# Seven half-size products for eight in the down projections of a two-layer encoder

## Chip, cores and metric

One Trainium2 chip, one core. The time is the device time of one execution in microseconds (us); of several runs the median is given. TensorE (PE in the profile) multiplies, VectorE is DVE, ScalarE is ACT, GpSimd is POOL, and SyncE (SP) here only issues transfers.

## What is computed

An encoder trunk of two layers is applied to two sequences of 512 and 256 tokens with the same weights; the kernel handles them side by side as 768 tokens of width 1024, in fp32. Each layer has an attention part and then a feed-forward part with a hidden width of 4096:

```python
for layer in range(DEPTH):                 # DEPTH = 2
    ...                                    # attention, residual add
    h = rmsnorm(x, ln_mlp[layer])
    x = x + jnp.square(jax.nn.relu(h @ w_up[layer])) @ w_down[layer]
return rmsnorm(x, ln_f)
```

The change concerns the second product of the last line, the down projection: 768 tokens x 4096 hidden features x 1024 outputs, once per layer.

## The kernel before

Activations lie with features on the 128 partitions and tokens along the columns: `x` is 8 tiles of 128 x 768. Every fp32 operand of a product is split into a high part of type fp32r (`hi`, a rounded copy by ScalarE) and the rest (`lo = src - hi`, a subtraction on VectorE): `wsplit` for weights (lines 78 to 81), `halve` for activations (lines 114 to 120). Each product is then three matmuls into the same PSUM accumulator: hi*hi, hi*lo, lo*hi. PSUM has 8 banks, 3 under the tag "mm" and 5 under "at" (`BANKS`).

`mlp(layer, ...)` holds the feed-forward part. Its up projection makes 16 pairs of hidden blocks (a block is 128 hidden features). The first two pairs are plain products. The other fourteen are made by the Strassen-Winograd scheme: tokens in two halves of 384 (`A`, `B`), input features in two halves, the two blocks of a pair as the third halving; seven products of half size in place of eight. The sums of weights that this needs are made by `weights` on GpSimd (line 866), the sums of activations once by `second` on VectorE (line 815), and the seven results are added to the outputs by VectorE (lines 889 and 952). `finish` applies ReLU, norm and square (lines 894 to 896), and the 16 results go to DRAM as `H`, of 128 x 2 x 768 each.

The down projection follows, the part that changes. The 32 hidden blocks are taken in four groups (`NG`) of eight (`GF`). For each group `read` loads the blocks two at a time on GpSimd's transfer queue (line 922) and splits them (`hp`). Then for each pair of output tiles (`mq`) two weight tiles of 128 x 1024 are loaded on SP's queue and split (`wtile`, lines 74, 80, 81), and for each output tile `proj_feat` (line 204) runs 8 blocks x 3 terms of a 512-column and a 256-column matmul (`dna`, `dnb`) on the same weights; VectorE adds both results to `x` (line 982). In layer 0's last group each finished tile of `x` is also split for the next layer and its square is summed. In layer 1 the last group is `final` (line 786): all outputs for the 512 tokens of the long sequence first, then, with the weights loaded and split a second time, for the other 256; each segment is normed, multiplied (line 795) and stored as soon as its eight tiles are there.

The kernel is written with a tile framework: buffers come from pools with a fixed number of slots per tag (`wraw` 3, `whi` and `wlo` 4 each), semaphores are added automatically, and the instructions of each engine are put into an order by a planner that follows the order in the program where several are ready. Once fixed, an engine's order is not changed on the chip: an instruction that waits holds up all behind it.

Of the kernel before, what the change touches and what calls it, by code (L numbers as in the profile page):

```python
# [17 lines left out]
P = 128  # L18
# [7 lines left out]
FF = 4 * D  # L26
NG = 4
GF = FF // P // NG
HT = NT // 2
MO = (0, 4, 1, 5, 2, 6, 3, 7)  # L30
MASKED = -3.0e38
# [6 lines left out]
def kernel(ctx: ExitStack, tc: tile.TileContext, a: dict, y: bass.AP):  # L38
# [75 lines left out]
    def halve(hi, lo, src, gain=None):  # L114
        if gain is None:
            nc.scalar.activation(hi, src, AF.Copy)  # L116
            nc.vector.tensor_tensor(out=lo, in0=src, in1=hi.bitcast(F32), op=ALU.subtract)  # L117
# [650 lines left out]

    def final(hs, x, sq):

        start = woff["w_down"]
        acc = cpool.tile([P, NT], F32, tag="acc", name="acc", bufs=1)
        R = cpool.tile([P, NT], F32, tag="R", name="R", bufs=1)
        for i, (s, e) in enumerate(SEGS):
            woff["w_down"] = start
            sl = slice(s, e)
            nm = Norm(sq, (s, e), acc)
            for mq in range(KD // 2):
                ws = [wtile("w_down", 1024) for _ in range(2)]
                for mi in range(2):  # L780
                    m = 2 * mq + mi
                    ps = ps_tile("mm", "fin")[:, : e - s]
                    lhs = down_lhs(ws, mi)
                    for k in range(GF):
                        for j, (part, mv) in enumerate(((0, hs[k][0]), (0, hs[k][1]), (1, hs[k][0]))):
                            nc.tensor.matmul(ps, lhs(k, part), mv[:, sl], start=(k == 0 and j == 0),  # L786
                                             stop=(k == GF - 1 and j == 2))
                    nc.vector.tensor_tensor(out=x[m][:, sl], in0=ps, in1=x[m][:, sl], op=ALU.add)
                    nm.add(x[m], KD - 1 if s else KD)
                    nc.scalar.activation(x[m][:, sl], x[m][:, sl], AF.Copy, scale=gcol(G_F, m))  # L790
            nm.spread(nm.rstd(), R)
            for k in range(KD):
                yt = x[k][:, sl]
                eng = nc.gpsimd if k % 3 == 1 else nc.vector
                eng.tensor_tensor(out=yt, in0=yt, in1=R[:, sl], op=ALU.mult)
                (nc.sync, nc.scalar)[k % 2].dma_start(y[:, k, sl], yt)

    def mlp(layer, src, o, x, es):

        g1s, g2s, st = ExitStack(), ExitStack(), ExitStack()
# [5 lines left out]
        A, B = slice(0, HT), slice(HT, NT)  # L808

        def put(pool, c, j, src, gain=None):  # L810
            t = comb[c, j] = pool.tile([P, 2, HT], F32R, tag=f"c{c}", name=f"c{c}", bufs=4)
            halve(t[:, 0], t[:, 1], src, gain)

        def stt(out, x_, s, y_, op):
# [2 lines left out]
        def first(j):  # L817

            for c, k, tk in ((1, j, B), (0, j, A), (2, j + 4, B), (3, j + 4, A)):
                put(g1, c, j, x[k][:, tk], gcol(g, k))  # L820

        def second():

# [13 lines left out]

        run(out_proj(src, o, None, x, 1, first))
        es.close()
        g2 = g2s.enter_context(tc.tile_pool(name="g2", bufs=4, side="right", reuse_waits="tile"))  # L840
        up = g2s.enter_context(tc.tile_pool(name="up", bufs=3, side="right", reuse_waits="tile"))

        def weights(plain=False):

# [7 lines left out]
            if plain:  # L852
# [7 lines left out]
            sa, sb = (up.tile([P, 1024], F32, tag="s", name="s", bufs=3) for _ in range(2))  # L860
# [53 lines left out]
        second()  # L914
        plain(both[1])

        hs = []

        def read(pool, f):

            hr = pa_.tile([P, 2, NT], F32, tag="hr", name="hr", bufs=2)
            nc.gpsimd.dma_start(hr, H[f // 2])  # L922
            for i in range(2):
                hp = pool.tile([P, 2, NT], F32R, tag="hp", name="hp")
                halve(hp[:, 0], hp[:, 1], hr[:, i])
                hs.append((hp[:, 0], hp[:, 1]))

        for mp in range(2, FF // 256):
            w = weights()
# [9 lines left out]
                rt = nm.rstd()  # L939
            if mp == FF // 256 - 1:  # L940

                g1s.close()
                pa_ = g1s.enter_context(tc.tile_pool(name=f"dna{layer}", bufs=4, reuse_waits="tile"))
                read(pa_, 0)
                read(pa_, 2)
            add(z12, one(6), z11)
            add(z11, p2, z11)
            p4 = one(4)
# [9 lines left out]
                    finish(wait.pop(0))  # L958
            finish(z)
        g2s.close()  # L960

        es = open_hl() if layer == 0 else None
        pb_ = st.enter_context(tc.tile_pool(name=f"dnb{layer}", bufs=6, reuse_waits="tile"))
        nxt, nn = [], Norm(sq)
        for grp in range(NG):
            if grp:
                hs = []
            for f in range(len(hs), GF, 2):
                read(pa_ if grp and f in (2, 4) else pb_, grp * GF + f)
            if layer == 1 and grp == NG - 1:  # L970
                final(hs, x, sq)
                st.close()
                g1s.close()
                return
            for mq in range(KD // 2):
                ws = [wtile("w_down", 1024) for _ in range(2)]
                for mi in range(2):
                    m = 2 * mq + mi
                    pa, pb = ps_tile("mm", "dna"), ps_tile("at", "dnb")
                    run(proj_feat(down_lhs(ws, mi), hs, GF, pa, pb))  # L980
                    xm = x[m]
                    evac_halves(pa, pb, lambda ps, s: nc.vector.tensor_tensor(out=xm[:, s], in0=ps, in1=xm[:, s], op=ALU.add))  # L982
                    if grp == NG - 1:
                        nxt.append(split(xm, "x", gcol(G_O, m)))
                        nn.add(xm)
        spill = dram.tile([P, KD, NT], F32, name="spill")
        for m in range(KD):
            nc.sync.dma_start(spill[:, m, :], x[m])
        st.close()
        g1s.close()  # L990
        return es, nxt, nn, spill


    hs_ = open_hl()
# [55 lines left out]
def _layout(i):  # L1050
# [40 lines left out]
    wd = i["w_down"].reshape(2, NG, 2, 4, P, D // 256, 256)  # L1091
    d["w_down"] = wd.transpose(0, 1, 5, 2, 4, 3, 6).reshape(-1)

    d["bias"] = _bias(i["rpb"][0])
    rep = lambda v: np.broadcast_to(v, (P, *v.shape))
# [39 lines left out]
```

## Time and profile before

| | |
|---|---|
| median of three runs | 1824.62 us (1824.50 to 1825.94) |
| the profiled execution | 1822.1 us, its span 1820.1 us |
| mean granted TensorE clock | 0.992 |
| TensorE / VectorE / ScalarE / GpSimd busy | 1777.1 / 1127.7 / 764.2 / 363.5 us |
| down projection of layer 0 | from 621.2 to 892.7 us of the span |
| down projection of layer 1, with the final norm | from 1532.9 us to the end |

A profile row names the line of the kernel, the engine, the operation, the tile written and the tiles read, the shape, and the count. In grouped rows the busy time and the mean duration in ns follow, then the idle time of the engine before such instructions with what ended it; rows by tile give least, median and greatest duration. Rows in order of time begin with the start in the span and the length in us; of several equal instructions in a row the length runs from the first start to the last end. Matmuls are pipelined: the distance of their starts counts, not their duration.

### The profile page before, as it was taken

The page shows a single profiled execution, that of the slowest core. Times are in us where ns is not written, and L with a number is a line of the kernel's source. Part 1 is how long each engine was busy: PE and PEld are TensorE (multiplying, and loading weights), DVE is VectorE, ACT ScalarE, POOL GpSimd, SP SyncE. Part 2 cuts the span into 40 slices and gives each one's busy share as a digit, 9 for nine tenths or more (in the row PEclk, how much of TensorE's full clock was granted, in tenths as well). Part 3 has the DMA queues.
Part 4 walks back from the last instruction along what each step waited for, and adds up shares of the span by engine and source line. Part 5 has one row for each costly group of instructions (what it writes and reads, how often), then busy time and mean ns, then how long its engine had stood idle before and what let it go on. Part 6 is the DMA issues. An engine that isn't in the chain of part 4 may idle for free.

```text
span 1820.1 us, 28502 instructions
## 1 busy us (share of the span) xinstructions
PE 1777.1 (98%) x11358; PEld 1627.3 (89%) x11358; DVE 1127.7 (62%) x2083; ACT 764.2 (42%) x1485; POOL 363.5 (20%) x366
## 2 busy tenths in 40 slices
PE   7999999999999999999999999999989999999997
PEld 7877888899999988888999999988989999888877
DVE  7777647497766634325366776775976667343255
ACT  6665534364434412213235555554544334122143
POOL 1421000014544200000022222210235442000002
PEclk8999999999999999999999999999999999999999
DMA  5111222313333634323211110122133336343233
GB/s 166 44 33 37 68 83 88 131 35 110 139 125 130 213 111 139 119 67 122 93 51 44 47 48 22 53 68 93 36 109 140 122 125 207 126 131 124 70 99 115
DMA packets 50019, 176.70 MB, mean 97 GB/s; under 512 B 5856, under 2 KB 8672, under 8 KB 49888
## 3 DMA queue, kind: packets, MB, share of 16 engines
q1 hardware_dynamic: 38656, 121.91, 21.2%
q0 software_dynamic: 4608, 25.17, 4.1%
q10 hardware_dynamic: 6624, 27.81, 3.9%
q8 instruction: 89, 1.46, 0.3%
q14 instruction: 42, 0.34, 0.1%
HBM read 142.63 MB, written 31.46 MB: 96 GB/s over the span
## 4 chain that ended last, share of the span: by engine, by line
PE 78%; DVE 8%; issue 8%; DMA 3%; ACT 3%; POOL 1%; DVEq 0%; SPq 0%; ACTq 0%; POOLq 0%
PE up L881 23%; PE dna L204 11%; PE dqk L192 8%; PE dnb L204 6%; PE opa L204 5%; PE dvp L192 4%; PE fin L786 3%; DMA hr<-H 2%; PE opb L204 2%; PE npa L204 2%; PE ds L270 2%; PE dpv L713 2%; DVE t L815 1%; PE vp L192 1%; PE qp L192 1%
## 5 line engine op out<-in xcount | busy, mean ns | idle before, releaser
L881 PE MATMUL up<-c,whi 128*128 128x384 f32 x1824 | 468.6, 338 | 5.8 <-ACT whi L80 5.8
L881 PEld LDWEIGHTS up<-c,whi 128*128 128x128 f32 x1824 | 331.9, 189 | 6.6 <-ACT whi L80 6.5
L204 PE MATMUL dna<-hp,whi 128*128 128x512 f32 x896 | 331.8, 394 | 1.1 <-DVE hp L117 0.9
L80 ACT ACTIVATE whi<-wraw 128x1024 fp32r<-128x1024 f32 (+2 forms) x200 | 193.3, 967 | 324.5 <-PE dnb L204 222.6
L881 PE MATMUL up<-c,wlo 128*128 128x384 f32 x912 | 308.1, 339 | 2.1 <-DVE wlo L81 2.1
L81 DVE TENSOR_TENSOR wlo<-wraw,whi 128x1024 fp32r<-128x1024 f32 (+2 forms) x204 | 228.4, 1121 | 98.9 <-ACT whi L80 98.7
L204 PE MATMUL dnb<-hp,whi 128*128 128x256 f32 x896 | 250.0, 283 | 0.0
L204 PEld LDWEIGHTS dna<-hp,whi 128*128 128x128 f32 x896 | 168.1, 188 | 42.1 <-DVE hp L117 1.9
L866 POOL TENSOR_TENSOR s<-wraw 128x512 f32<-128x512 f32 x56 | 94.1, 1699 | 414.9 <-DMA wraw<-in_w_up_dram 199.8
L204 PE MATMUL dna<-hp,wlo 128*128 128x512 f32 x448 | 176.6, 394 | 0.0
L881 PEld LDWEIGHTS up<-c,wlo 128*128 128x128 f32 x912 | 172.2, 189 | 2.9 <-DVE wlo L81 2.9
L204 PEld LDWEIGHTS dnb<-hp,whi 128*128 128x128 f32 x896 | 167.2, 188 | 0.3
L889 DVE TENSOR_TENSOR z<-up,z 128x384 f32<-128x384 f32 x168 | 92.9, 553 | 90.4 <-PE up L881 79.0
L982 DVE TENSOR_TENSOR x<-dna,x 128x512 f32<-128x512 f32 x56 | 38.7, 691 | 165.6 <-PE dna L204 165.4
L204 PE MATMUL dnb<-hp,wlo 128*128 128x256 f32 x448 | 126.9, 283 | 0.0
L192 PE MATMUL dqk<-whi,xh 128*128 128x256 f32 x384 | 114.7, 299 | 0.0
L192 PE MATMUL dqk<-whi,xl 128*128 128x256 f32 x384 | 107.5, 280 | 0.0
L192 PE MATMUL dqk<-wlo,xh 128*128 128x256 f32 x384 | 107.2, 279 | 0.0
L922 POOL DMA_DIRECT2D hr<-H x32 | 17.6, 550 | 431.6 <-DVE hp L117 390.8
L204 PEld LDWEIGHTS dna<-hp,wlo 128*128 128x128 f32 x448 | 84.1, 188 | 18.3
L80 ACT ACTIVATE whi<-s 128x1024 fp32r<-128x1024 f32 x56 | 59.5, 1063 | 84.8 <-PE up L881 83.5
L116 ACT ACTIVATE hp<-hr 128x768 fp32r<-128x768 f32 x64 | 50.9, 837 | 100.2 <-PE dnb L204 61.8
(214 smaller groups left out, 3892.7 us busy)
## 6 DMA issues: line engine op xcount, KB each, us to landing
wraw<-in_w_down_dram SPq DMA_DIRECT2D x72, 512.0 KB, 3.6
wraw<-in_w_up_dram SPq DMA_DIRECT2D x64, 512.0 KB, 3.5
H<-z ACTq DMA_DIRECT2D x32, 768.0 KB, 3.3
hr<-H POOLq DMA_DIRECT2D x32, 768.0 KB, 5.9
wraw<-in_w_in_o_dram SPq DMA_DIRECT2D x24, 512.0 KB, 3.6
wraw<-in_w_in_e_dram SPq DMA_DIRECT2D x16, 512.0 KB, 3.7
x<-in_xT_dram SPq DMA_DIRECT2D x16, 384.0 KB, 5.4
nbias<-in_bias_dram SPq DMA_DIRECT2D x20, 256.0 KB, 3.8
```

Of the source, the lines that this page charges most:

```text
L80: nc.scalar.activation(hi, raw, AF.Copy)
L81: nc.vector.tensor_tensor(out=lo, in0=raw, in1=hi.bitcast(F32), op=ALU.subtract)
L116: nc.scalar.activation(hi, src, AF.Copy)
L192: nc.tensor.matmul(ps[:, :256], st[:, tk], col(k, part, 0, 256), start=(k == 0 and i == 0), stop=(k == KD - 1 and i == 2))
L204: nc.tensor.matmul(ps[:, : e - s], w, mv[:, s:e], start=(k == 0 and i == 0), stop=(k == nk - 1 and i == 2))
L270: nc.tensor.matmul(out[h], q(a_, hp, qs), k(b_, hp, ks), start=i == 0, stop=i == 2)
L713: nc.tensor.matmul(pv, pt[:, i * P : (i + 1) * P], v[:, k0 // P + i, vc], start=(i == 0), stop=(i == nk - 1))
L786: nc.tensor.matmul(ps, lhs(k, part), mv[:, sl], start=(k == 0 and j == 0), stop=(k == GF - 1 and j == 2))
L866: nc.gpsimd.tensor_tensor(out=d_, in0=x_, in1=y_, op=ALU.add)
L881: nc.tensor.matmul(ps, part[a_][:, base + k * P : base + (k + 1) * P], t[:, b_], start=q + k + i == 0, stop=q == n - 1 and k == 3 and i == 2)
L889: nc.vector.tensor_tensor(out=out, in0=x_, in1=y_, op=op)
L982: evac_halves(pa, pb, lambda ps, s: nc.vector.tensor_tensor(out=xm[:, s], in0=ps, in1=xm[:, s], op=ALU.add))
```

## The change

Per layer, hidden pairs 0, 1 and 14, 15 (the first and last four blocks) stay plain, with half as many blocks per output tile as before. The other twelve pairs, n = 0 to 11 for H[2] to H[13], go in four groups (`SG`) of three (`SJ`) by the seven-product scheme, now with the two blocks of a pair as the summed halving, the token halves, and two output tiles.

- `pair` loads the two blocks (two transfers on SP's queue), makes four sums of 128 x 384, and splits seven operands (three of 384, two of 768 that hold two operands each). The sums are on GpSimd for the first group and on VectorE afterwards. Buffers hold five pairs, so that two of the next group's three can be made while a group is in use.
- `down_weights` loads two tiles of 128 x 768, makes four sums of 128 x 384 on GpSimd, and splits four tiles (768, 384, 768, 768).
- `down_pair` runs the seven products, each summed in PSUM over the group's three pairs and the three terms (9 matmuls of 384 columns), in the order 1, 2, 6, 5, 7, 3, 4. Accumulator `u` takes 1, and after copies or reads also 6, 7 and 4; `v` takes 5 and then 3; `r` takes 2. ScalarE copies two intermediate results (`keep`), VectorE adds five to `x` from PSUM, GpSimd adds the two copies.
- Loads of `H` move from GpSimd's queue to SP's, in two halves.
- `final` has four blocks instead of eight and keeps the split weights for its second segment.
- Pools are opened and closed in another order to make room; the weight layout in DRAM follows the new order of use.

```diff
+SJ = 3
+SG = (FF // 256 - 4) // SJ
...
     def final(hs, x, sq):
...
-                ws = [wtile("w_down", 1024) for _ in range(2)]
+                if i == 0:
+                    kept.append([wtile("w_down", 1024)])
+                ws = kept[mq]
...
-                    for k in range(GF):
+                    for k in range(len(hs)):
...
+        hrp = st.enter_context(tc.tile_pool(name=f"hr{layer}", bufs=4, reuse_waits="tile"))
...
-            hr = pa_.tile([P, 2, NT], F32, tag="hr", name="hr", bufs=2)
-            nc.gpsimd.dma_start(hr, H[f // 2])
+        def load(mp):
+            hr = [hrp.tile([P, NT], F32, tag="h", name="hr", bufs=4) for _ in range(2)]
             for i in range(2):
+                nc.sync.dma_start(hr[i], H[mp][:, i])
+            return hr
...
+        def pair(n, eng):
+
+            low = n % 5 > 2
+            hr = load(n + 2)
+            b11, b12, b21, b22 = hr[0][:, A], hr[0][:, B], hr[1][:, A], hr[1][:, B]
+            t = pa_.tile([P, 3, HT], F32, tag="t", name="dt", bufs=1)
+            n6, n7, t4 = (t[:, i] for i in range(3))
+
+            def small(src, scale=None):
+                c = (pa_ if low else ph_).tile([P, 2, HT], F32R, tag="c3", name="c3", bufs=6 if low else 9)
+                halve(c[:, 0], c[:, 1], src, scale)
+                return c[:, 0], c[:, 1]
+
+            def large(pool, bufs, src):
+                c = pool.tile([P, 2, NT], F32R, tag="c6", name="c6", bufs=bufs)
+                halve(c[:, 0], c[:, 1], src)
+                return [(c[:, 0, h], c[:, 1, h]) for h in (A, B)]
+
+            d = ops[n] = {1: small(b12, -1.0)}
+            eng.tensor_tensor(out=n7, in0=b11, in1=b21, op=ALU.subtract)
+            eng.tensor_tensor(out=b11, in0=b12, in1=b11, op=ALU.subtract)
+            eng.tensor_tensor(out=n6, in0=b21, in1=b11, op=ALU.add)
+            eng.tensor_tensor(out=t4, in0=b22, in1=n6, op=ALU.subtract)
+            d[3], d[2] = large(*((pa_, 4) if low else (pm_, 3)), hr[1])
+            d[6], d[7] = large(*((pa_, 4) if low else (ph_, 3)), t[:, :2].rearrange("p a t -> p (a t)"))
+            d[5] = small(b11)
+            d[4] = small(t4)
+
+        def down_weights():
+
+            w = SJ * P
...
+            sa = xo_tile("s")
+            sb = pa_.tile([P, NT], F32, tag="s", name="s", bufs=1)
...
+            for ps_, t in (((1, 4), raws[0]), ((2,), raws[1]), ((6, 5), sa), ((7, 3), sb)):
+                if t is sa:
+                    for d_, x_, y_ in ((s1, a21, a22), (s2, s1, a11), (s3, a11, a21), (s4, a12, s2)):
+                        nc.gpsimd.tensor_tensor(out=d_, in0=x_, in1=y_, op=ALU.add)
+                hi, lo = whilo(w * len(ps_))
+                wsplit(hi, lo, t[:, : w * len(ps_)])
...
+        def down_pair(g, q, w):
+
+            xs1, xs2 = x[2 * q], x[2 * q + 1]
+            x11, x12, x21, x22 = xs1[:, B], xs1[:, A], xs2[:, B], xs2[:, A]
+            u, v, r = ps_tile("at", "du")[:, :HT], ps_tile("at", "dv")[:, :HT], ps_tile("mm", "dr")[:, :HT]
+
+            def prod(ps, n, start):
+                part, base = w[n]
+                for j in range(SJ):
+                    c = ops[g * SJ + j][n]
+                    for i, (a_, b_) in enumerate(((0, 0), (0, 1), (1, 0))):
+                        nc.tensor.matmul(ps, part[a_][:, base + j * P : base + (j + 1) * P], c[b_],
+                                         start=start and j + i == 0, stop=j == SJ - 1 and i == 2, skip_group_check=not start)
+
+            def keep(ps, scale):
+                t = ph_.tile([P, HT], F32, tag="pk", name="pk", bufs=2)
+                nc.scalar.activation(t, ps, AF.Copy, scale=scale)
+                return t
+
+            def put(xd, ps, op=ALU.add, eng=nc.vector):
+                eng.tensor_tensor(out=xd, in0=xd, in1=ps, op=op)
+
+            prod(u, 1, True)
+            p1 = keep(u, -1.0)
+            prod(r, 2, True)
+            prod(u, 6, False)
+            put(x12, u, ALU.subtract)
+            put(x11, r)
+            put(x11, p1, eng=nc.gpsimd)
+            prod(v, 5, True)
+            p5 = keep(v, -1.0)
+            prod(u, 7, False)
+            put(x22, u)
+            put(x22, p5, eng=nc.gpsimd)
+            prod(v, 3, False)
+            put(x12, v)
+            prod(u, 4, False)
+            put(x21, u)
...
+        plain_down(hs, lambda xm, m: None)
+        w = down_weights()
+        for n in range(SJ):
+            pair(n, nc.gpsimd)
+        for g in range(SG):
+            for q in range(KD // 2):
+                down_pair(g, q, down_weights() if g + q else w)
+            if g < SG - 1:
+                for n in range((g + 1) * SJ, (g + 2) * SJ):
+                    pair(n, nc.vector)
+        hs = []
+        for mp, pools in ((14, ((pm_, 3), (pa_, 4))), (15, ((pa_, 4), (pa_, 0)))):
+            read(mp, pools, hs)
```

`plain_down` is the former loop over output tiles with four blocks, and `read` now fills the plain blocks' operands from `load`.

More of the change, by code (lines that the diff above doesn't have):

```diff
@@ L859, in weights @@
                 return out
[L860 removed]
+            sa, sb = (us.tile([P, 1024], F32, tag="s", name="s", bufs=3) for _ in range(2))
             s2, s1, s3, s4 = (r[:, i * 512 : (i + 1) * 512] for r in (sa, sb) for i in range(2))
@@ new lines, in read @@
+        def read(mp, pools, hs):
+            hr = load(mp)
+            for i, (pool, bufs) in enumerate(pools):
+                if bufs:
+                    hp = pool.tile([P, 2, NT], F32R, tag="c6", name="c6", bufs=bufs)
+                    hi, lo = hp[:, 0], hp[:, 1]
+                else:
+                    hi, lo = (pool.tile([P, 2, HT], F32R, tag="c3", name="c3", bufs=6).rearrange("p a t -> p (a t)") for _ in range(2))
+                halve(hi, lo, hr[i])
+                hs.append((hi, lo))
@@ L940, in mlp @@
             if mp == FF // 256 - 1:
+                uss.close()
                 g1s.close()
                 pa_ = g1s.enter_context(tc.tile_pool(name=f"dna{layer}", bufs=4, reuse_waits="tile"))
-                read(pa_, 0)
-                read(pa_, 2)
+                hs = []
+                for mp_ in range(2):
+                    read(mp_, ((pa_, 4), (pa_, 4)), hs)
             add(z12, one(6), z11)
@@ L960, in mlp, with plain_down @@
         g2s.close()
[L962 to L974, printed above, removed]
+        pm_ = ms.enter_context(tc.tile_pool(name=f"dnm{layer}", bufs=3, reuse_waits="tile"))
+        ph_ = bs.enter_context(tc.tile_pool(name=f"dnh{layer}", bufs=3, reuse_waits="tile"))
+        def plain_down(hs, then):
             for mq in range(KD // 2):
-                ws = [wtile("w_down", 1024) for _ in range(2)]
+                ws = [wtile("w_down", 1024)]
                 for mi in range(2):
```

74 lines of the change are left out of this document (51 added, 23 removed).

## The prediction

> **What bounds the kernel now.** I read the page's shares first, then the chain that ended last, then busy times by stretch, then groups by shape, then the order in time where VectorE and GpSimd are busy at once.
>
> ```profile
> span 1820.1 us, 28502 instructions
> PE 1777.1 (98%) x11358; PEld 1627.3 (89%) x11358; DVE 1127.7 (62%) x2083; ACT 764.2 (42%) x1485; POOL 363.5 (20%) x366
> PE 78%; DVE 8%; issue 8%; DMA 3%; ACT 3%; POOL 1%; DVEq 0%; SPq 0%; ACTq 0%; POOLq 0%
> ```
>
> TensorE is busy 98% of the span and carries 78% of the last chain, so fewer columns through TensorE are worth their time as long as nothing else becomes late. The next view gives busy times in pieces of the first up, first down, second up and second down projection (length, then busy time and count for each engine).
>
> ```profile
> core 0: us, PE busy (x) PEld busy (x) DVE busy (x) ACT busy (x) POOL busy (x), PEclk, DMA share, GB/s
> 450.00:600.00 150.00, 150.00 (x861) 150.00 (x860) 104.61 (x122) 60.39 (x62) 79.80 (x43) 1.00 0.38 129
> 640.00:760.00 120.00, 120.00 (x678) 104.79 (x677) 46.83 (x62) 26.70 (x29) 4.32 (x8) 1.00 0.33 107
> 1360.00:1520.00 160.00, 160.00 (x917) 160.00 (x917) 112.68 (x134) 63.16 (x65) 81.38 (x44) 1.00 0.37 127
> 1540.00:1700.00 160.00, 159.83 (x910) 139.81 (x909) 62.49 (x80) 38.64 (x42) 5.94 (x11) 1.00 0.39 126
> ```
>
> The down stage has TensorE full at clock 1.00, VectorE 39% busy (46.83 of 120) and GpSimd idle: TensorE alone bounds it. The up stage already runs seven products for eight, with VectorE at 70% and GpSimd at 53%, and TensorE still never stops. That is the nearest sight of what the down stage will become.
>
> **The change, part by part.**
>
> *TensorE.* A 384-column product takes 150/861 = 0.1742 or 160/917 = 0.1745 us: 0.1743. A down product is a 512 and a 256 column one together: 2 x 120/678 = 0.354 or 2 x 160/910 = 0.3516, mean 0.3528. Per layer 24 of 32 blocks change. Before: 24 blocks x 8 output tiles x 3 terms = 576 pairs x 0.3528 = 203.2 us. After: 4 groups x 4 column pairs x 7 products x 3 block pairs x 3 terms = 1008 x 0.1743 = 175.7 us. Gain 27.5 per layer, 55.0 in all. The eight plain blocks keep their columns. [...]
>
> *VectorE and ScalarE.* Durations by shape (mean ns after the busy time, or least/median/most), and runs of equal instructions, which give the pitch:
>
> ```profile
> L81 DVE TENSOR_TENSOR wlo<-wraw,whi 128x1024 fp32r<-128x1024 f32 x152 | 185.7, 1223 | 97.9 <-ACT whi L80 97.8
> L117 DVE TENSOR_TENSOR hp<-hr,hp 128x768 fp32r<-128x768 f32 x64 | 58.8, 954 | 46.1 <-ACT hp L116 45.7
> L117 DVE TENSOR_TENSOR c<-t,c x32: 544/551/1655, 384.4 to 1317.9; 128x384 fp32r<-128x384 f32 x32
> L889 DVE TENSOR_TENSOR z<-up,z x168: 542/552/559, 423.1 to 1538.6; 128x384 f32<-128x384 f32 x168
> L116 ACT ACTIVATE hp<-hr 128x768 fp32r<-128x768 f32 x64 | 50.9, 837 | 100.2 <-PE dnb L204 61.8 <-DMA hr<-H 30.2 <-DMA H<-z 7.3
> 384.39 1.96 DVE L117 TENSOR_TENSOR c<-t,c 128x384 fp32r<-128x384 f32 x4
> 621.50 1.82 DVE L117 TENSOR_TENSOR hp<-hr,hp 128x768 fp32r<-128x768 f32 x2
> L936 ACT ACTIVATE z<-up x28: 470/493/495, 416.8 to 1520.5; 128x384 f32<-128x384 f32 x28
> ```
>
> Four 384-wide ones in 1.96 us, the last taking 0.55: pitch (1.96 - 0.55)/3 = 0.47. Two of 768 in 1.82: pitch 0.87 (1.82 less one of 0.95). Call a step one `down_pair` with its weights: 63 products, 10.98 us of TensorE, 16 per layer. VectorE per step: weight splits of 768, 384, 768, 768 = 3.08; five additions out of PSUM (552 ns as the 384 split's 551) 5 x 0.47 = 2.35. Per pair of hidden blocks: three 384 splits, two 768 splits, four additions = 3 x 0.47 + 2 x 0.87 + 4 x 0.47 = 5.03. Nine of twelve pairs are made during the first twelve steps, 0.75 per step, 3.77. Together 9.20 of 10.98 us, 84%: it fits, with little room. ScalarE per step: splits 3 x 0.84 + 0.49, two `keep` 0.98, pairs 0.75 x (3 x 0.49 + 2 x 0.84) = 2.4, in all 6.4: not the bound.
>
> *GpSimd.* Four weight sums and two additions into `x` per step, all 384 wide.
>
> ```profile
> 568.66 1.30 POOL L866 TENSOR_TENSOR s<-wraw,s 128x512 f32<-128x512 f32 x1
> L674 POOL TENSOR_TENSOR rope_o<-t,t x48: 457/462/1285, 915.4 to 1195.2; 128x128 f32<-128x128 f32 x48
> ```
>
> Undisturbed it takes 1.30 us for 512 columns and 0.46 for 128, so about 1.02 for 384: 6.1 of 10.98 us. Alone it fits too.
>
> *The two together.* This is what decides. GpSimd and VectorE take turns:
>
> ```profile
> 386.26 4.79 DVE L815 SCALAR_TENSOR_TENSOR t<-x,gains,t 128x384 f32<-128x384 f32 x3
> 385.26 3.81 POOL L866 TENSOR_TENSOR s<-wraw 128x512 f32<-128x512 f32 x2 [191.01 <-ACT c L116]
> 389.03 1.61 POOL L866 TENSOR_TENSOR s<-s,wraw 128x512 f32<-128x512 f32 x1
> L815 DVE SCALAR_TENSOR_TENSOR t<-x,gains,t x32: 600/611/1658, 381.7 to 1313.8; 128x384 f32<-128x384 f32 x32
> L152 DVE TENSOR_TENSOR acc<-acc,sq 128x512 f32<-128x512 f32 x7 | 4.8, 688 | 2.1 <-ACT sq L147 2.1
> 1789.65 6.38 DVE L795 TENSOR_TENSOR x<-x,R 128x512 f32<-128x512 f32 x5
> 1789.76 5.12 POOL L795 TENSOR_TENSOR x<-x,R 128x512 f32<-128x512 f32 x3 [2.08 <-DVE R L182]
> ```
>
> Three VectorE instructions with both inputs in SBUF took 4.79 us, 1.60 each where 0.61 is usual, and in the same time GpSimd made about one per 1.60. Additions that read PSUM (L889) never stretched: 542 to 559 ns over 168. So a GpSimd 512 occupies what both need for 1.60 - 0.47 = 1.13 us; in the last stage's multiplications, 512 wide (free 0.69, pitch 0.61), for (6.38 - 5 x 0.61 - 0.08)/3 = 1.08. With 1.10, a 384 takes 0.83 by columns. Per step: VectorE with two SBUF inputs 3.08 + 3.77 = 6.85, GpSimd 6 x 0.83 = 5.0, sum 11.85, above TensorE's 10.98. If GpSimd's turns all fall under the PSUM additions or idle time of VectorE the step is 11.85; if none do, 6.85 + 2.35 + 5.0 = 14.2. From below, the up stage shows the turns nearly free:
>
> ```profile
> 563.78 0.86 DVE L81 TENSOR_TENSOR wlo<-wraw,whi 128x512 fp32r<-128x512 f32 x1
> 565.14 2.28 DVE L894 SCALAR_TENSOR_TENSOR z<-z,R 128x1536 f32<-128x1536 f32 x1
> 607.80 0.69 DVE L81 TENSOR_TENSOR wlo<-wraw,whi 128x512 fp32r<-128x512 f32 x1
> 608.99 1.76 DVE L894 SCALAR_TENSOR_TENSOR z<-z,R 128x1536 f32<-128x1536 f32 x1
> ```
>
> Beside the sums 0.86 and 2.28, without them 0.69 and 1.76: 0.69 us lost to four GpSimd instructions. But there the two add to 3 x 1.22 + 0.69 + 1.76 + 4 x 1.10 = 10.5 us in 84 products (14.6 us), 72%; here to 108% of the step. I take 12.4, near the lower end: the weight sums have several us before their splits are due, and the PSUM additions give them 2.35 us. Cost 12 x (12.4 - 10.98) = 17.0 per layer. The last four steps make no pairs (3.08 + 0.87 for the late plain blocks + 5.0 = 8.95) and stay with TensorE.
>
> *First plain stage.* 96 pairs of products, 33.9 us. Beside it GpSimd makes 16 instructions (16.3) and VectorE the splits of three pairs (9.5), of plain blocks and weights (11): some 37 us in turns, and product 6, the first that needs a sum, starts 3.1 us late enough to allow 37. Between 0 and 5 per layer; I take 1.
>
> *DMA.* Blocks and weights come on SP's queue. A step moves 0.77 MB of weights and 0.75 x 0.79 MB of blocks in 12 us, 113 GB/s, as the 107 to 126 above: nothing. A block load now stands ahead of weight loads in the same queue and waits for its buffer; it delays weights only if the pair before is late, which 12.4 holds already.
>
> *The end.*
>
> ```profile
> 1734.74 6.10 DMA hr<-H
> 1741.75 43.60 PE fin L786 x198
> PE fin L786 <- ACT hp L116: 1.8, 1, 1.8
> 1799.35 10.00 PE fin L786 x82
> ```
>
> Late blocks cost the last stage 1.8 us, which go, since they are now read a group ahead; so do the second loads and splits of the weights. Against it the second segment shrinks to 96 x 10.00/82 = 11.7 us, over which the five VectorE and three GpSimd multiplications (6.38 us) must still fit: 0 to +2. I take -2 in all.
>
> *Sum.* -55.0 + 34.0 + 2 - 2 = -21. The profiled execution took 1822.1 us (span 1820.1 and 2.0 around it) and would take 1801; the median of the runs is 2.5 higher, so 1803.
>
> **The rivals.**
>
> *It is all hidden.* As in the up stage TensorE never waits: the step stays 10.98 and the time is 1824.6 - 57 = 1768. For it: VectorE 84% and GpSimd 56% each fit. Against it: 11.85 in turns.
>
> *PSUM accumulators alone.* `u` takes product 6 on top of 1 after ScalarE's copy, product 7 after VectorE has read it, and 4 after that; behind product 6 stands only product 5, 1.57 us, of which the addition takes 0.55. A VectorE instruction of 0.95 just begun leaves nothing. If turns are free but this costs 0.3 us at two places of 32 steps, 19 us: 1787.
>
> *VectorE pays for every turn (slower).* The step reaches 14.2 in twelve of sixteen: 12 x 3.22 = 38.6 lost per layer against 27.5, +22 in all, 1847. It decides from 10.98 + 27.5/12 = 13.3 on. For it: with VectorE full its next instruction is a two-input one in 11 of 16 cases, and 1.60 for 0.61 above is just that. [...]
>
> **How the numbers follow.** Turns at 12 to 13.3 per step: 0.45, of which 0.05 within 0.2% of now. All hidden 0.15; accumulators alone 0.10; slower 0.30, of which 0.03 ends within 0.2%. That bound, 0.2% or 3.6 us, is what a measurement here can tell from no change. Faster 0.65, same 0.08, slower 0.27. The likeliest case spans 1790 to 1825. For 8 in 10 the range goes down towards 1768 and up half-way and more to 1847: 1772 to 1838.
>
> **What would show it.** TensorE's pace per 384 columns of the new products, 0.174, confirms the first term; the length of a stretch of four steps gives the step (44 us hidden, 50 as forecast, 57 in the slow case). Sums and `x` additions on GpSimd stretched to 1.4 us or more, and two-input VectorE instructions of 384 columns at 1.4 instead of 0.55, show the turns; TensorE waiting for VectorE's additions before products 7 and 4 shows the accumulators. Waits on weight splits would say that the queue order, not the turns, is at fault. The prediction is wrong if the turns cost under 5 us per layer, or if stops stand at the borders of groups only.

## The result and the profile after

The changed kernel is slower: 1851.33 us (1850.39 to 1854.02) against 1824.56 us for the kernel before on the same chip, ratio 1.0154 [1.0132, 1.0177]. The profiled execution took 1850.4. The forecast was 1803 (1772 to 1838); the time is close to that of the rival that ended on the other side, 1847. One execution of the kernel without pair sums, below, took 2220 us at a granted clock of 0.706, and its ratio leaves it out.

The totals of the profile after, the span's line, busy times, and the shares of the chain that ended last:

```profile
span 1848.5 us, 29045 instructions
PE 1756.8 (95%) x11070; PEld 1644.4 (89%) x11070; DVE 1373.5 (74%) x2395; ACT 864.3 (47%) x1693; POOL 639.3 (35%) x550
PE 74%; DVE 18%; ACT 3%; issue 2%; POOL 2%; DMA 1%; DVEq 0%; ACTq 0%; SPq 0%; POOLq 0%
```

TensorE fell from 98 to 95% of a longer span, and VectorE's share of the last chain rose from 8 to 18%. By stretch, the down projection of layer 0 took 283.1 us (622.6 to 905.7) where it took 271.5, and that of layer 1 with the end 301.9 (from 1546.6) where it took 287.2; the rest moved by 2.1 in all. In layer 0 the plain blocks at both ends took 33.7 us each, so the whole loss is in the seven products between them. Busy times of that section in both layers (length, then busy time and count by engine, granted clock, DMA):

```profile
core 0: us, PE busy (x) PEld busy (x) DVE busy (x) ACT busy (x) POOL busy (x), PEclk, DMA share, GB/s
656.30:872.00 215.70, 191.41 (x1010) 184.56 (x1009) 185.96 (x231) 92.02 (x144) 123.20 (x92) 0.95 0.31 95
1580.30:1796.50 216.20, 190.69 (x1010) 183.85 (x1010) 186.02 (x230) 91.95 (x145) 123.19 (x92) 0.95 0.30 92
```

1008 products at 0.1743 us are 175.7 us, so each section is 40 us too long. Two things are to be seen: TensorE stands still for some 25 us of it, and the granted clock is 0.95, not 1.00. TensorE's waits in the whole span (total us, times, longest):

```profile
PE du L1003 <- DVE x L1012: 39.0, 31, 2.9
PE du L1003 <- ACT pk L1008: 9.6, 2, 5.0
PE dv L1003 <- ACT pk L1008: 1.0, 3, 0.4
```

The 31 waits are for VectorE's read of accumulator `u` (`put`, now line 1012), about one per step. VectorE's rows in order of time show why the read is late; this is the sixth step of layer 0, with VectorE, GpSimd and TensorE in turn:

```profile
730.01 1.57 DVE L83 TENSOR_TENSOR wlo<-s,whi 128x768 fp32r<-128x768 f32 x1
731.51 1.38 DVE L119 TENSOR_TENSOR c<-dt,c 128x384 fp32r<-128x384 f32 x1
732.81 1.36 DVE L122 SCALAR_TENSOR_TENSOR c<-hr,c 128x384 fp32r<-128x384 f32 x1
734.09 1.37 DVE L960 TENSOR_TENSOR dt<-hr 128x384 f32<-128x384 f32 x1
735.50 0.56 DVE L961 TENSOR_TENSOR hr<-hr 128x384 f32<-128x384 f32 x1
735.97 0.55 DVE L1012 TENSOR_TENSOR x<-x,dr 128x384 f32<-128x384 f32 x1
736.43 0.95 DVE L83 TENSOR_TENSOR wlo<-wraw,whi 128x768 fp32r<-128x768 f32 x1
737.30 0.55 DVE L1012 TENSOR_TENSOR x<-x,du 128x384 f32<-128x384 f32 x1
...
729.76 1.01 POOL L985 TENSOR_TENSOR s<-wraw 128x384 f32<-128x384 f32 x1 [0.95 <-DVE wlo L83]
730.85 1.62 POOL L985 TENSOR_TENSOR s<-s,wraw 128x384 f32<-128x384 f32 x1
732.42 1.33 POOL L985 TENSOR_TENSOR s<-wraw 128x384 f32<-128x384 f32 x1
733.71 1.33 POOL L985 TENSOR_TENSOR s<-wraw,s 128x384 f32<-128x384 f32 x1
...
734.94 0.33 PE L1003 MATMUL dv<-c,wlo 128*128 128x384 f32 x1
737.90 0.62 PE L1003 MATMUL du<-c,whi 128*128 128x384 f32 x2 [2.63 <-DVE x L1012]
```

While GpSimd makes its four weight sums, VectorE needs 5.49 us (730.01 to 735.50) for four instructions whose undisturbed pitches add to 2.28 (0.87 + 3 x 0.47): 3.21 us lost, 0.80 per sum. Behind them, in VectorE's fixed order, stand `x<-x,dr` (the last matmul of its product starts at 731.78, the addition at 735.97), a split of 0.95, and only then the read of `u` for which product 7 waits. TensorE starts nothing between 734.94 and 737.90. VectorE's reads of `u` in PSUM are not stretched, 537 to 555 ns, as the prediction had it (least, median and greatest duration in ns, whole span):

```profile
L1012 DVE TENSOR_TENSOR x<-x,du x96: 537/546/555, 670.1 to 1797.1; 128x384 f32<-128x384 f32 x96
```

VectorE also waits. Its busy time in the first twelve steps of layer 0, and its waits for TensorE's products in them:

```profile
core 0: us, PE busy (x) PEld busy (x) DVE busy (x) ACT busy (x) POOL busy (x), PEclk, DMA share, GB/s
656.30:824.90 168.60, 146.15 (x758) 140.45 (x757) 151.79 (x191) 73.67 (x118) 97.19 (x72) 0.94 0.32 97
```

```profile
DVE x L1012 <- PE du L1003: 5.4, 4, 2.5
DVE x L1012 <- PE dv L1003: 4.2, 4, 1.2
DVE x L1012 <- PE dr L1003: 1.1, 1, 1.1
```

VectorE is busy 12.65 us per step (151.79/12) and idle for 1.4 more, most of it waiting for TensorE, which at other times waits for VectorE: a step is longer than the work of either.

### The profile page after: what moved, and what is told of

Its sections match the earlier page's. It is cut to its first block, busy times and chain, and to the rows that moved or that the text cites. A ratio compares the mean times of both kernels' runs of the same rounds, so it can differ in the third digit from the quotient of the medians.

```text
span 1848.5 us, 29045 instructions
## 1 busy us (share of the span) xinstructions
PE 1756.8 (95%) x11070; PEld 1644.4 (89%) x11070; DVE 1373.5 (74%) x2395; ACT 864.3 (47%) x1693; POOL 639.3 (35%) x550
## 4 chain that ended last, share of the span: by engine, by line
PE 74%; DVE 18%; ACT 3%; issue 2%; POOL 2%; DMA 1%; DVEq 0%; ACTq 0%; SPq 0%; POOLq 0%
PE up L886 22%; PE du L1003 8%; PE dqk L194 7%; PE opa L206 5%; DVE c L119 4%; PE dv L1003 4%; PE dvp L194 4%; DVE wlo L83 4%; PE opb L206 2%; PE npa L206 2%; PE ds L272 2%; PE dpv L715 2%; PE dr L1003 2%; PE fin L789 2%; DVE x L1012 1%
## 5 line engine op out<-in xcount | busy, mean ns | idle before, releaser
L1003 PE MATMUL du<-c,whi 128*128 128x384 f32 x768 | 208.0, 353 | 48.7 <-DVE x L1012 39.0
L1003 PEld LDWEIGHTS du<-c,whi 128*128 128x128 f32 x768 | 141.6, 194 | 60.9 <-DVE x L1012 50.2
L82 ACT ACTIVATE whi<-s 128x768 fp32r<-128x768 f32 (+1 forms) x120 | 113.5, 946 | 172.9 <-PE up L886 86.5
L83 DVE TENSOR_TENSOR wlo<-s,whi 128x768 fp32r<-128x768 f32 (+1 forms) x120 | 147.1, 1228 | 22.2 <-ACT whi L82 21.4
L1003 PE MATMUL du<-c,wlo 128*128 128x384 f32 x384 | 133.3, 347 | 0.0
L1012 POOL TENSOR_TENSOR x<-x,pk 128x384 f32<-128x384 f32 x64 | 87.1, 1361 | 113.1 <-DVE x L1012 100.9
L1003 PE MATMUL dv<-c,whi 128*128 128x384 f32 x384 | 105.6, 358 | 1.1 <-ACT pk L1008 1.0
L985 POOL TENSOR_TENSOR s<-wraw 128x384 f32<-128x384 f32 x64 | 79.2, 1238 | 75.5 <-DVE wlo L83 75.2
L700 ACT ACTIVATE de<-ds,m 128x512 f32<-128x512 f32 (+1 forms) x96 | 58.4, 613 | 81.2 <-DVE m L698 81.2
L901 ACT ACTIVATE z<-z 128x1536 f32<-128x1536 f32 x32 | 47.6, 1491 | 71.6 <-DVE z L899 71.6
```

The lines of the kernel that those rows point to most:

```text
L82: nc.scalar.activation(hi, raw, AF.Copy)
L83: nc.vector.tensor_tensor(out=lo, in0=raw, in1=hi.bitcast(F32), op=ALU.subtract)
L700: nc.scalar.activation(e, s, AF.Exp, bias=m, scale=1.0, accum_out=l2[:, c : c + 1])
L985: nc.gpsimd.tensor_tensor(out=d_, in0=x_, in1=y_, op=ALU.add)
L1003: nc.tensor.matmul(ps, part[a_][:, base + j * P : base + (j + 1) * P], c[b_], start=start and j + i == 0, stop=j == SJ - 1 and i == 2, ski ...
L1012: eng.tensor_tensor(out=xd, in0=xd, in1=ps, op=op)
```

## Experiments

A is the theory that the turns of GpSimd and VectorE cost the time; its rival B, that VectorE has simply too much to do, so that more work on it would make the kernel slower still. A third, C, is the prediction's rival on accumulators: that the order of the products leaves too little room before the reads of the accumulators. "Section" is the time from the first to the last of the 1008 products of a layer, layer 0 / layer 1; "step" one `down_pair`. Ratios are to the kernel before, with 95% intervals.

**Without the weight sums.** The four GpSimd sums of each step are left out; the same splits read the raw weights.

```diff
...
-            for ps_, t in (((1, 4), raws[0]), ((2,), raws[1]), ((6, 5), sa), ((7, 3), sb)):
-                if t is sa:
-                    for d_, x_, y_ in ((s1, a21, a22), (s2, s1, a11), (s3, a11, a21), (s4, a12, s2)):
-                        nc.gpsimd.tensor_tensor(out=d_, in0=x_, in1=y_, op=ALU.add)
+            for ps_, t in (((1, 4), raws[0]), ((2,), raws[1]), ((6, 5), raws[0]), ((7, 3), raws[1])):
```

> Leaves out the four GpSimd sums of weights in each down step and splits the loaded weights a second time instead, so VectorE, ScalarE and TensorE keep every instruction; only GpSimd's 4 of 6 instructions per step go. Theory A (GpSimd and two-input VectorE instructions take turns; 6 turns of 0.83 us per step): the excess of the seven-product section over its 175.7 us (now 40 us per layer) falls by more than half, section 185 to 195 us, time 1795 to 1810. Theory B (VectorE has too much of its own to do): section stays near 216, time 1851. Theory C (TensorE waits because product 7 follows too closely on the read of its accumulator): stays above 205, time above 1830.

1786.23 us, 0.9797 [0.978, 0.9814]. The busy times of the two sections of this kernel:

```profile
core 0: us, PE busy (x) PEld busy (x) DVE busy (x) ACT busy (x) POOL busy (x), PEclk, DMA share, GB/s
657.50:840.60 183.10, 179.49 (x1010) 176.72 (x1010) 148.47 (x227) 91.36 (x144) 45.72 (x32) 1.00 0.37 115
1549.00:1732.30 183.30, 179.59 (x1011) 176.68 (x1010) 149.38 (x227) 91.52 (x144) 44.88 (x32) 1.00 0.37 112
```

VectorE executes the same instructions as in the changed kernel, and is busy 148 us where it was 186; most steps are 11.1 us. So the weight sums carry 65 us of the time, more than A said, and the TensorE term is there once they are gone. The 37.5 us of VectorE's busy time are some 0.6 per sum (60 fall in a section), less than the 0.80 of the sixth step, where all four fell beside two-input instructions.

**Additions to `x` from PSUM on VectorE.** The other GpSimd work of a step goes, and ScalarE's two copies with it.

```diff
-            p1 = keep(u, -1.0)
+            put(x11, u, ALU.subtract)
...
-            put(x11, p1, eng=nc.gpsimd)
...
-            p5 = keep(v, -1.0)
+            put(x22, v, ALU.subtract)
...
-            put(x22, p5, eng=nc.gpsimd)
```

> The two additions per step that ScalarE copies out of PSUM and GpSimd adds to x are made by VectorE straight from PSUM. GpSimd loses two turns of 0.83 us, VectorE gains two instructions of 0.47 us. Theory A: a step gains about 1.66 - 0.94 = 0.7 us where VectorE is full, 8 us per layer, time 1835. Theory B: VectorE has 0.94 us per step more, 11 to 15 us per layer, time 1875 to 1880. Theory C: one more read of u before product 6, time 1851 or more.

1824.69 us, 1.0013 [1.0001, 1.0024]; sections 203.0 / 203.2. VectorE got two more instructions per step and the kernel 27 us faster, against B and by more than A said (1835).

**No pair sums on VectorE.** The sums of the blocks in the second to fourth group are left out, and the splits read the blocks themselves.

```diff
+            if n < SJ:
...
+            else:
+                s67, t4 = hr[0], b22
```

> Leaves out VectorE's four pair sums in the second to fourth group (the loaded halves are split in their place); GpSimd's six instructions per step stay. VectorE loses 4 x 0.47 x 0.75 = 1.41 us per step of the first twelve. Theory A in its sum form (VectorE's two-input work and GpSimd's turns add up): 14.06 - 1.41 to 12.6 per step, about 17 us per layer, time 1815 to 1825. If GpSimd's turns cost the same however much VectorE has to do (they stretch the instructions around its reads of u): less than 5 us per layer, 1840 to 1850.

1816.27 us, 0.9955 [0.9941, 0.9969]; sections 197.8 / 199.9. Taking three two-input instructions per step from VectorE gains 35 us, about what A's sum of both engines' times says: either side of the turns may be lightened.

**Turns, or the splits' wait for the sums?** Four kernels take the two apart. First, the kernel without sums gets four GpSimd instructions per step that only write (into tiles that nothing reads):

```diff
...
+                nc.gpsimd.memset(d_, 1.0)
...
```

> As the version without weight sums (1786 us), but GpSimd fills the four 128 x 384 tiles of each step with a constant: as many GpSimd instructions as in the changed kernel, which write SBUF and read nothing from it, and whose result nobody uses. If GpSimd being busy or writing is what hinders VectorE: above 1810. If only its reading of SBUF hinders: 1784 to 1792.

then four sums that read SBUF, into the same unread tiles:

```diff
...
+                nc.gpsimd.tensor_tensor(out=d_, in0=x_, in1=x_, op=ALU.add)
...
```

> As the version without weight sums (1786 us), but GpSimd makes four sums of 128 x 384 per step from the loaded weights into tiles that nobody reads. Nothing waits for these sums. If the turns alone cost the time: 1830 to 1851, near the changed kernel. If the cost was that the splits waited for late sums: near 1786.

The first: 1784.21 us, 0.9797 [0.978, 0.9813]. The second: 1821.3 us, 0.9995 [0.9986, 1.0004]. The group of the four in the first (count, busy us, mean ns, idle time before):

```profile
L981 POOL MEMSET s<- 128x384 f32 x128 | 50.3, 419 | 40.1 <-PE up L886 20.1 <-DVE acc L154 16.9
```

And in the second:

```profile
L981 POOL TENSOR_TENSOR s<-wraw 128x384 f32<-128x384 f32 x128 | 143.5, 1142 | 118.1 <-DMA wraw<-in_w_down_dram 118.1
```

The section of layer 0 in the first:

```profile
core 0: us, PE busy (x) PEld busy (x) DVE busy (x) ACT busy (x) POOL busy (x), PEclk, DMA share, GB/s
651.90:835.50 183.60, 179.67 (x1010) 176.58 (x1009) 149.01 (x228) 91.35 (x143) 45.27 (x32) 1.00 0.38 115
```

The memsets wait for nothing, and all 128 ran ahead of the sections: this line counts 32 GpSimd instructions, the additions to `x` alone. So the 1784 us do not show what writing beside the steps would cost. The trace does where the memsets ran; here is a split of VectorE beside them, and the same split beside a sum that reads, in the kernel without weight sums:

```profile
420.92 5.92 POOL L981 MEMSET s<- 128x384 f32 x14
422.36 1.23 DVE L83 TENSOR_TENSOR wlo<-s,whi 128x1024 fp32r<-128x1024 f32 x1 [1.91 <-ACT whi L82]
...
428.29 1.30 POOL L871 TENSOR_TENSOR s<-wraw 128x512 f32<-128x512 f32 x1 [2.58 <-DMA wraw<-in_w_up_dram]
428.48 2.19 DVE L83 TENSOR_TENSOR wlo<-s,whi 128x1024 fp32r<-128x1024 f32 x1 [1.91 <-ACT whi L82]
```

It takes 1.23 us beside GpSimd instructions that only write and 2.19 beside one that reads. The unread sums do run beside the steps, and cost 35 us (1786 to 1821) though nobody waits for their results. TensorE, VectorE and ScalarE execute the instructions of a section in the same order with them and without, so no other order explains it: these are the turns by themselves, with the clock of 0.50 that went with some of the waits, 10.2 us of it per section (last section).

Third, the change's own four sums, in their chain and place, but with the splits reading the raw weights:

```diff
-            for ps_, t in (((1, 4), raws[0]), ((2,), raws[1]), ((6, 5), sa), ((7, 3), sb)):
-                if t is sa:
+            for ps_, t in (((1, 4), raws[0]), ((2,), raws[1]), ((6, 5), raws[0]), ((7, 3), raws[1])):
+                if 6 in ps_:
```

> The changed kernel's four GpSimd sums per step, with their operands, their order one behind the other and their place in the program, but the splits read the loaded weights, so that nothing waits for a sum (the unused sums that did not hang on each other gave 1821, no sums 1786). If the remaining 30 us of the changed kernel came from splits that waited for late sums: near 1821 again. If they came from where in the step the sums fall (beside VectorE's additions): 1840 to 1855.

1836.86 us, 1.0077 [1.0056, 1.0097]; sections 208.7 / 209.7, between the two expected values. So of the 65 us, 35 are turns of sums that come at once with the weights' arrival, some 15 more come with the sums in a chain behind the first two splits, and some 14 with the splits' wait for them; each of the last two is known to about 5 us, each part holds its share of the slow clock, and for the last part VectorE's order differs in places too.

Fourth, more room: order 1, 5, 6, 2, 3, 7, 4, with an accumulator of its own for product 4, and the weight sums split a place earlier.

```diff
             prod(u, 1, True)
             p1 = keep(u, -1.0)
-            prod(r, 2, True)
+            prod(v, 5, True)
+            p5 = keep(v, -1.0)
             prod(u, 6, False)
...
+            prod(r, 2, True)
...
+            prod(v, 3, False)
+            put(x12, v)
             prod(u, 7, False)
...
-            prod(u, 4, False)
             put(x21, u)
+            r4 = ps_tile("mm", "dr")[:, :HT]
+            prod(r4, 4, True)
+            put(x21, r4)
```

> The changed kernel with the products of a step in the order 1, 5, 6, 2, 3, 7, 4 and product 4 in an accumulator of its own: two products (3.1 us) in place of one stand between product 6 and product 7, which waits for VectorE's read, and product 4 waits for no read. VectorE makes one PSUM addition more per step (0.47 us); GpSimd's work is as in the changed kernel. Theory C (lateness of VectorE costs only where the order gives it a single product of slack): waits before product 7 mostly gone, section from 216 to 190 to 200, time 1800 to 1825. Theory A alone (VectorE and GpSimd in turns are slower than TensorE over the whole step): 0.47 us more per step, time 1845 to 1865.

1840.31 us, 1.0093 [1.0074, 1.0112]. 11 us gained: less than C said, and faster than A alone said. The waits of this kernel:

```profile
PE du L1003 <- DVE x L1012: 28.2, 16, 3.0
PE du L1003 <- ACT pk L1008: 15.7, 6, 5.5
```

Half as many waits for the read of `u` as before, but longer ones on average, and more for ScalarE's copies: lateness shows elsewhere.

**The rest of the change.** The twelve pairs are again plain products, two pairs per group, with all else of the change kept (loads of `H` on SP's queue, four blocks and kept weights in `final`, pools); the weight layout follows.

```diff
+        for g in range(6):
+            hs = []
...
+            plain_down(hs, lambda xm, m: None)
```

> No seven-product scheme in the down projections: all 16 pairs plain in stages of four blocks, with everything else of the change (blocks loaded on SP's queue in halves, four-block stages, the final stage with four blocks and kept weights). If these parts cost nothing, the time is that of the kernel before within 4 us (1819 to 1827); if the finer stages or the final stage cost something, it is that much above. The forecast had a gain of 2 us here.

1822.41 us, 1.0006 [0.9996, 1.0016]: no gain and no loss to be seen, as expected if these parts cost nothing.

**Where to put the sums.** The same four weight sums on VectorE:

```diff
-                        nc.gpsimd.tensor_tensor(out=d_, in0=x_, in1=y_, op=ALU.add)
+                        nc.vector.tensor_tensor(out=d_, in0=x_, in1=y_, op=ALU.add)
```

> The four sums of weights per step move from GpSimd to VectorE, which is the busier engine: 4 x 0.47 = 1.88 us more for it. Theory A: each sum took a turn of 0.83 us and now takes 0.47, so a step of the first twelve gets 1.4 us shorter at most, time 1815 to 1835. Theory B: 1.88 us per step more on the bottleneck, time 1890 to 1910.

1796.85 us, 0.9853 [0.9833, 0.9873]: faster than A said, and B, which said slower than now, is refuted. The waits of this kernel, and one section:

```profile
PE du L1003 <- ACT pk L1008: 7.6, 2, 4.0
PE du L1003 <- DVE x L1012: 4.5, 12, 0.7
```

```profile
core 0: us, PE busy (x) PEld busy (x) DVE busy (x) ACT busy (x) POOL busy (x), PEclk, DMA share, GB/s
657.40:848.00 190.60, 183.23 (x1010) 178.99 (x1009) 179.81 (x292) 91.33 (x144) 47.36 (x32) 0.98 0.35 108
```

VectorE has 61 instructions more than in the changed kernel (292 against 231) and is busy 6 us less. The waits for `u` fell from 39.0 to 4.5 us. About half of what is left stands in the first step (17.9 / 16.6 us); the others take 11.1 to 12.6.

Both edits together, `x` additions and weight sums on VectorE:

```diff
+                        nc.vector.tensor_tensor(out=d_, in0=x_, in1=y_, op=ALU.add)
...
+            put(x11, u, ALU.subtract)
...
+            put(x22, v, ALU.subtract)
```

> Both moves together: GpSimd does nothing in the steps, VectorE has 9.20 + 1.88 + 0.94 = 12.0 us per step in the first twelve and 8.3 in the last four. Theory A: steps of 12.0 to 12.5 in place of 14.06, section 191 to 200 us, time 1800 to 1820, faster than either move alone. Theory B: 2.8 us per step more, time above 1900.

1810.8 us, 0.9935 [0.9911, 0.9959]: slower than the weight sums alone, which A did not say. Most steps are 11.1 us, but the first, ninth and thirteenth, each the first of a group, 15.9 to 19.1.

Weight sums and also the first group's pair sums on VectorE:

```diff
-            pair(n, nc.gpsimd)
+            pair(n, nc.vector)
```

> As the version with the weight sums on VectorE (section 190 us, of which the first step takes 17 to 18 us), and the pair sums of the first group, made by GpSimd beside the first plain stage, are on VectorE too. Theory A (turns): in that stage VectorE no longer lags behind, so ScalarE's first copy is in time; the first step falls from 17 to below 13 us, section 184 to 186, time 1783 to 1790. Rival (the first step waits because ScalarE's queue has the next pairs' splits ahead of the copy, whatever the lag): first step stays at 16 to 18, time 1795 to 1800.

1806.96 us, 0.992 [0.9906, 0.9935], a miss. The first step is 11.3 / 11.8 as expected, but the ninth 14.6 / 16.1 and the thirteenth 17.6 / 16.6, with waits for ScalarE's weight splits that were 2.0 us in all before:

```profile
PE du L1003 <- ACT whi L82: 10.5, 4, 3.5
```

The reordered products, as in their diff above, together with the weight sums on VectorE:

```diff
+                        nc.vector.tensor_tensor(out=d_, in0=x_, in1=y_, op=ALU.add)
```

> The order with more slack and the weight sums on VectorE, which alone gave 1797. With the turns gone there was little wait left before product 7 (4.5 us in all), so at best 5 us better; the additional PSUM addition costs VectorE 0.47 us per step. 1790 to 1805; above 1810 if VectorE (now 11.5 of 10.98 us in the first twelve steps) becomes the bound.

1815.55 us, 0.9968 [0.9956, 0.998], a miss too: 11.1 us in most steps, 16.7 to 19.3 in the first, ninth and thirteenth. In these three kernels the ninth and thirteenth steps wait for splits of weights, VectorE's or ScalarE's. VectorE's, in this kernel and in the one with both edits:

```profile
PE du L1003 <- DVE wlo L83: 11.1, 2, 5.6
PE du L1003 <- DVE wlo L83: 7.5, 4, 2.2
```

Why these splits came late there was not settled, nor what stalls the first step where it stays long.

Only the last, or the last two, of the first group's three pairs on VectorE, besides the weight sums:

```diff
-            pair(n, nc.gpsimd)
+            pair(n, nc.vector if n == SJ - 1 else nc.gpsimd)
```

> As the version with the weight sums on VectorE (1797, first step of each layer 17 to 18 us), and of the first group's three pairs the last one's four sums are on VectorE too, eight stay on GpSimd. If the first step waits because GpSimd's late turns at the end of the plain stage keep VectorE behind: first step 11 to 14, time 1785 to 1795. If it is the planner's order of the later steps that takes it back, as with all twelve sums moved (first step 11.3, the 9th and 13th 14.6 and 17.6): 1797 to 1808.

```diff
-            pair(n, nc.gpsimd)
+            pair(n, nc.vector if n else nc.gpsimd)
```

> The same with two of the three pairs' sums on VectorE and four sums on GpSimd. First step 11 to 13; by the turns 1785 to 1792, by the planner's order 1797 to 1808.

1792.93 us, 0.9837 [0.9823, 0.9852], and 1796.94 us, 0.9862 [0.9845, 0.9878], the second between its two expected ranges. Sections of the first:

```profile
core 0: us, PE busy (x) PEld busy (x) DVE busy (x) ACT busy (x) POOL busy (x), PEclk, DMA share, GB/s
653.20:840.80 187.60, 180.99 (x1010) 176.24 (x1009) 178.84 (x291) 90.78 (x143) 48.38 (x32) 1.00 0.36 112
1549.80:1738.10 188.30, 182.54 (x1011) 177.92 (x1010) 179.22 (x290) 91.07 (x144) 47.05 (x32) 0.99 0.35 108
```

It beats both kernels, the one before by 1.6%. Its first step takes 14.5 / 15.0 us, a little over the 11 to 14 expected. Against the weight sums alone on VectorE its interval overlaps, so that the last edit gains is not shown. The second has a first step of 11.5 / 11.1, but its other steps, 11.1 to 13.2, give that back.

## Why the prediction was wrong

- **TensorE's term was right.** Without weight sums a section takes 183.1 us where 175.7 was the sum, and that kernel is 37 us faster than the one before, the 55 less twice 7 and a few us elsewhere.
- **The price of a turn was near, the step's length was not.** 0.83 us per GpSimd instruction was forecast; four sums cost VectorE 0.80 each in the sixth step and some 0.6 in the mean of a section, and the sign named for the turns came (two-input instructions of 384 columns at 1.36 to 1.38 us). What failed is "I take 12.4, near the lower end", with its reason that the weight sums have several us before their splits are due and that the PSUM additions give them 2.35 us. The first twelve steps of layer 0 are 14.06 us in the mean (distance of first products, 168.7/12). VectorE's busy time in them, 12.65 per step, is close to the 12.4; the prediction took it for the length of the step, and left out that VectorE and TensorE wait for each other in turn and that the clock was at 0.50 after most of the longer waits. The slack of the sums does not help: what they hold up is not only their own splits but VectorE's other work, in a fixed order with the read of `u` at its end. Unread sums, with all the slack there is, still cost 35 us. With the measured excess of the two sections the sum comes out: -55.0 + 40.0 + 40.5 = +25.5 of the 27 measured.
- **The slow rival had the size and half the mechanism.** Its 14.2 meant a VectorE without idle time, and in the twelve steps that it speaks of VectorE was idle for 16.8 of 168.6 us. That 14.06 is within 1% of 14.2 is in part luck: the first step, 19.7 us by what the plain stage left behind, stands in the mean, and without it the other eleven are 13.5. The length came from late reads of `u`, 1.2 us of wait per step (39.0/32), from ScalarE's copies, 9.6 us in all, in the two first steps, and from the clock (below). That those reads are where it shows was the rival on accumulators; that they are not the cause, the reordered kernel (11 us) and the kernel without sums (65 us) show.
- **The last four steps were forecast at TensorE's pace.** They are 47.1/4 = 11.8 us, 3 us per layer lost, 2 of them in the thirteenth step, which took 13.3 us and 11.1 without the weight sums. With the sum of VectorE's and GpSimd's times at 8.95 of 10.98 us the turns were not free either.
- **The first plain stage.** The stage itself is 33.7 us as forecast, but VectorE leaves it late: the first steps took 19.7 and 19.2 us. With two of three pairs' sums moved they fell from 17.9 / 16.6 to 11.5 / 11.1, so the sums of pairs beside the plain stage delay some 6 us per layer, not 1 and not within its 0 to 5; in the total that gain did not appear.
- **DMA and end.** DMA delayed nothing that the waits show. (A step's weights are 0.79 MB, not 0.77, which changes nothing.) The forecast -2 for the end is not there: the rest of the change gave 0 (1.0006). The last plain segments of layer 1, four blocks from 1796.5 to 1837.4 us, took 40.9 where 33.7 is their TensorE time, 7.2 lost; eight blocks before lost 6.2.
- **The clock was missing from the prediction.** It is a second loss behind most of the longer waits: 20.5 us of each section at 0.50, at most some 10 us lost per layer.

## What to carry to other kernels

Before giving work to an idle GpSimd, compare what its instruction takes from VectorE with what VectorE would need to do it: here some 0.6 us in the mean, and 0.80 where every sum met a two-input instruction, against a pitch of 0.47, so that the "idle" engine made VectorE slower than the work itself would. Add up both engines' two-input times; where the sum is over TensorE's, expect a step longer than the stretched work of VectorE too, since both engines wait for each other (here 14.06 us for 12.65). More room before the reads of accumulators brought only 11 us here. Price a long stop of TensorE with the slow clock too: in the changed kernel nine of the ten stops of 2.1 us and more went with 3.4 or 6.8 us at a clock of 0.50.

## What the runs showed of the hardware

After most of the longer waits TensorE ran at a granted clock of 0.50. Around the step shown above, in pieces (before the wait, the wait, after it):

```profile
core 0: us, PE busy (x) PEld busy (x) DVE busy (x) ACT busy (x) POOL busy (x), PEclk, DMA share, GB/s
728.00:734.90 6.90, 6.90 (x41) 6.90 (x40) 6.90 (x7) 2.19 (x3) 5.87 (x5) 1.00 0.23 79
734.90:739.20 4.30, 1.67 (x10) 1.36 (x9) 4.27 (x8) 1.03 (x2) 1.73 (x2) 0.99 0.19 41
739.30:742.50 3.20, 3.20 (x11) 2.87 (x11) 3.17 (x6) 1.44 (x4) 0.89 (x1) 0.50 0.81 264
742.60:776.00 33.40, 30.54 (x169) 29.26 (x169) 29.38 (x35) 15.99 (x25) 20.50 (x17) 1.00 0.29 87
```

From 739.3 to 742.5 the granted clock is 0.50 and 11 products start where 18 would. In each section of the changed kernel such stretches, 3.4 or 6.8 us long, add to 20.5 us, in which 61 and 54 products start where 20.5/0.1743 would be 117 (the stretches from 664.0 and 1585.6 us begin before the stop has ended): some 10 us per layer, a quarter of the excess, and less if VectorE caught up meanwhile. There nine of the ten stops of 2.1 us and more (from start to start of the products around them) went with one, and none of the stops up to 1.96 us; after the tenth, 2.29 us long and from 1701.1 us on, the clock stayed at 1.00. The two longest, 5.38 and 4.86 us, went with 6.8 us each. The length of a stop does not settle it: the tenth is longer than one of 2.11 us that went with a stretch, and in the kernel without pair sums one of 2.10 us did and one of 3.57 did not. Per section the stretches add to nothing without the weight sums or with memsets, to 10.2 us with unread sums, 6.8 with the `x` additions on VectorE, and 6.8 / 3.4 with the weight sums on VectorE: up to 20 of the 65 us of the weight sums came by way of the clock.
